# A macaron diffusion layer: side work of the first FFN handed out in small pieces, and the right-hand pools moved by 288 bytes

## The chip, the cores and the metric

One core of a Trainium2 chip runs the whole layer as one program. The metric is the device time of one execution in microseconds (us); three timed runs of the kernel before gave a median of 2588.1 us.

## What is computed

One layer works on 1024 latent tokens and 256 context tokens with 1024 features, all in float32: a half-step SwiGLU, then attention and a state-space branch (S5) side by side, then a second half-step SwiGLU for the latents, then a final norm. Each part is preceded by an RMS norm with a shift and a scale, and followed by a gate; the nine shift, scale and gate vectors come from a small product with the conditioning vector (adaLN).

```python
def swiglu(h, w_gu, w_down):
    gate, up = jnp.split(h @ w_gu, 2, axis=-1)
    return (jax.nn.silu(gate) * up) @ w_down
...
x = x + 0.5 * mx[2] * swiglu(modulate(x, g_ffn1[l], mx[0], mx[1]), w_gu1[l], w_down1[l])
ctx = ctx + 0.5 * mc[2] * swiglu(modulate(ctx, g_ffn1[l], mc[0], mc[1]), w_gu1[l], w_down1[l])
```

The S5 branch needs tables that depend on parameters alone (powers of the state matrix, input and output matrices). They can be made at any time before that branch.

## The kernel before

Every float32 product is made of three matmuls (mm3, L572): each operand is split into a high and a low part, and high x high, high x low and low x high are added in PSUM. ACT makes the high part, POOL the low part (split, L568).

**The first FFN** (ffn, L593) holds the transposed, normed tokens in three blocks: 512, 512 and 256 tokens (XB). Its hidden width of 2816 is walked in 22 slices f of 128. A slice does the gate product of all three blocks, then the up product of all three; a block of 512 is 24 matmuls of 512 columns, the third block 24 of 256. ACT takes the silu of a gate block out of PSUM (silu, L655), VectorE (DVE) multiplies the up block with it (act_of, L661), ACT and POOL split the result. The down products run at every second slice for two slices at once, between the gate and the up products: ten token tiles of 128, two halves each, six matmuls a half (120 in a phase), and DVE adds each half to the accumulator acc in SBUF (accum, L647). There are four PSUM banks with the tag gu and four with the tag dn. Slice 21 does the down products of slice 20 alone, three matmuls a half. The instructions of an engine run in program order.

**The side work.** A generator (gen in ffn1_mix_in, L820) makes, on DVE and POOL, the later adaLN vectors (adaln_rest, L178) and then the S5 tables (s5_pre, L246): small arithmetic first, then 16 cells (8 pairs of groups, 2 directions). A cell has six products on DVE (AB), six on POOL (M), a copy (rep), and the table T with 32 DVE operations. side (L581) advances the generator by one step, twice a slice: ahead of the gate products, and ahead of the up products. One step is four adaLN weight rows, or a whole cell. What needs PSUM and TensorE (PE) is put off with defer (L578): reduce and extract of adaLN, and finish of a cell (transposes s5p and products s5k on two dn banks, copies and some 17 DMA issues on ACT's queue); it runs at a later call of side.

**Scaling of the accumulator.** At slice 20, behind its down products, at (L829) multiplies all ten accumulator tiles by the gate (DVE), adds the input to five of them on POOL and, behind the up products, to the other five on DVE. From there on the down weights are multiplied by the gate when they are loaded (load, L599).

**Where the tiles lie.** Pools open from the left (upwards from address 0, where 1024 bytes are kept for DMA) or from the right (downwards). The allocator of the program of before gives these start addresses, in bytes of a partition: left, the weights of FFN 1 (78528, 82624, ...), the activations (53952, ...), FFN 2's first token block hH0, hL0 (45760, 62144) and its weights (87744, ...): all leave 192 when divided by 512. Right: big (147424), FFN 2's second token block hH1, hL1 (196576, 212960) and w_glu (133088): all leave 480. The tile big holds the tokens of FFN 1, later the keys and latents of attention, and both operands of the product with w_out (wo).

Of the kernel before, what the change touches and what calls it, by code (L numbers as in the profile page):

```python
# [41 lines left out]
XB = [(0, 4), (4, 4), (8, 2)]  # L42


class Kernel:
# [30 lines left out]
    def build(self):  # L76
        with self.tc.manual_schedule(), ExitStack() as st:
# [7 lines left out]
            sbig, srow, sattn = ExitStack(), ExitStack(), ExitStack()  # L85
            self.big = self.pool(sbig, "big", side="right").tile([128, 80 * 256], F32R, name="big")
# [91 lines left out]
    def adaln_rest(self, pool):  # L178
# [36 lines left out]
        def reduce(chunk, s, acc):  # L215
            p = [self.bank("dn", "adp") for _ in range(2)]
            for h in range(2):
                nc.tensor.matmul(p[h], lhsT=self.ones, rhs=acc[:, h * 512:(h + 1) * 512], start=True, stop=True)
            self.defer(0, lambda: extract(chunk, s, p))

        accs, grow = None, {}
        for i, (chunk, kt) in enumerate(jobs):
            sets = (0, 1) if chunk <= 4 else (0,)
            if i % 4 == 0:
                yield 5.0 * len(sets)
# [13 lines left out]
            if kt == KT - 1:  # L239
                for s in sets:  # L240
                    self.defer(0, lambda chunk=chunk, s=s, acc=accs[s]: reduce(chunk, s, acc))
        while self.late:
            yield 1.0


    def s5_pre(self, st):  # L246
# [14 lines left out]
        with ExitStack() as s0:  # L261
# [11 lines left out]
            def exp_parts(x, w, em=False):  # L273
# [5 lines left out]
                self.ts(q, r, 1.0 / 8, MUL, 1.0, ADD)  # L279
                for i in (7, 6, 5, 4, 3, 2):  # L280
                    self.tt(q, q, r, MUL)
                    self.ts(q, q, 1.0 / i, MUL, 1.0, ADD)
                self.tt(q, q, r, MUL)
# [10 lines left out]
            yield 6.0  # L294
            ld = sm("e4", 1)
            self.ts(ld[:, 0], par[:, 2, :], -87.0, ALU.max, 88.0, ALU.min)
            dt, _ = exp_parts(ld, 1)
# [10 lines left out]
            mg, em = exp_parts(x, 2, True)  # L308
            mag, em1 = mg[:, 0], em[:, 0]
            V.tensor_copy(self.r8, mg[:, 1])  # L310
            yield 6.0
# [11 lines left out]
            self.ts(v, t2, -1.0 / 132, MUL, 1.0, ADD)  # L323
            for ds, dv in ((72, 90), (42, 56), (20, 30), (6, 12)):
# [3 lines left out]
                self.ts(v, v, -1.0 / dv, MUL, 1.0, ADD)  # L328
            self.tt(s, s, th, MUL)
            self.tt(v, v, t2, MUL)  # L330
            self.ts(v, v, 0.5, MUL)
            for _ in range(2):
# [5 lines left out]
                self.ts(s, t, 2.0, MUL)  # L338
            cs = sm()
# [13 lines left out]
            V.reciprocal(out=den, in_=den)  # L353
            self.tt(fr, am1, lr, MUL)
# [7 lines left out]
            yield 6.0  # L362
# [7 lines left out]
            yield 6.0  # L370
# [8 lines left out]
            while m < NSEQ:  # L379
# [12 lines left out]
                m *= 2  # L392
            dv = lambda x: x.rearrange("p r t (c d g) -> p r t d c g", d=2, g=GC)
# [13 lines left out]

        for c in range(G // GC):
            mk = []
            for d in range(2):  # L410
                yield 6.4 if d else 7.8
                if d == 0:
# [7 lines left out]
                    tb = pool.tile([128, 2 * GC, CH], F32, tag="tb", name="tb")  # L420
                    self.ts(bW, bW, sgn, MUL)
# [3 lines left out]
                    self.tt(B2, bW, b8(fr), MUL)  # L425
                    self.tt(tb, bS, b8(fi), MUL)
                    self.tt(B2, B2, tb, SUB)
                    self.ts(C1, C1, sgn, MUL, -1.0, MUL)
                    self.ts(C2, C2, -1.0, MUL)
                gq = slice((c * 2 + d) * GC, (c * 2 + d + 1) * GC)  # L430
# [8 lines left out]
                def cross(nt, p, X, Y, first, second, tag, e):  # L439
                    ta = buf("ta" + tag, GC * 9 * CH, GC, nt, CH)  # L440
                    o1 = buf("o1" + tag, GC * 9 * CH, GC, nt, CH)
                    o2 = buf("o2" + tag, GC * 9 * CH, GC, nt, CH)
                    self.tt(o1, pv(p, 0, nt), bv(X, nt), MUL, e)
                    self.tt(ta, pv(p, 1, nt), bv(Y, nt), MUL, e)
                    self.tt(o1, o1, ta, ADD, e)
                    self.tt(o2, pv(p, first[0], nt), bv(first[1], nt), MUL, e)
                    self.tt(ta, pv(p, second[0], nt), bv(second[1], nt), MUL, e)
                    self.tt(o2, o2, ta, SUB, e)
                    return o1, o2
# [10 lines left out]
                for r in range(2):  # L460
                    V.tensor_copy(T[:, r, :, col(0, NB)], bsrc[:, r] if d == 0 else bsrc[:, r, :, ::-1])
                for l in range(5):
# [4 lines left out]
                             bb(lev[:, l, 0]), bb(lev[:, l, 1]), T[:, 0, :, col(m, m + ln)], T[:, 1, :, col(m, m + ln)])  # L467

# [35 lines left out]
                self.defer(0, finish)  # L504
# [10 lines left out]
            self.defer(2, fin2)  # L515
        while self.late:
            yield 1.0
# [60 lines left out]
    def defer(self, slots, fn):  # L578
        self.late.append([slots, fn])

    def side(self, budget):  # L581
        late, self.late = self.late, []
        for e in late:
            if e[0] <= 0:
                e[1]()
            else:
                self.late.append([e[0] - 1, e[1]])
        if self.gen is not None and self.cost <= budget:
            self.cost = next(self.gen, None)
            if self.cost is None:  # L590
                self.gen = None

    def ffn(self, blocks, hT, w_gu, w_dn, acc, P, hook=None, side=None, at=None, preload=None, keep=False, joint=False, start=None, pairs=0):  # L593
# [40 lines left out]
        def down(fs, tiles, post):  # L634
            for t in tiles:
                b = next(i for i, (t0, n) in enumerate(blocks) if t0 <= t < t0 + n)
                ts = slice((t - blocks[b][0]) * 128, (t - blocks[b][0] + 1) * 128)
                for half in range(2):
# [6 lines left out]
                    post(t, cs, p)  # L645

# [33 lines left out]
        for f in range(NF):  # L680
# [46 lines left out]
    def ffn1_mix_in(self, srow):  # L727
# [23 lines left out]
        with ExitStack() as sact:  # L751
            actp = self.pool(sact, "act")
            with ExitStack() as sw:
# [72 lines left out]
                self.gen, self.cost = gen(), 0.0  # L826
# [925 lines left out]
```

## Time and profile before

| | us |
|---|---|
| median of three runs | 2588.1 |
| lowest, highest | 2588.07, 2588.35 |
| the profiled execution's own time | 2585.26 |
| its span, first to last instruction | 2583.5 |

PE is busy for 2450.9 us of the span, DVE for 1580.0, POOL for 1091.8 and ACT for 810.9. The first FFN runs from about 62 to 1070 us of the span, the mixing part to 1830 (attention from about 1250), the second FFN to the end. In the profile a name before the arrow is the tile written, those behind it are the tiles read; L59 is the helper of all tensor_tensor operations, L574 to L576 are the three matmuls of mm3. The granted clock is given as a share of full speed.

### The profile page before, as it was taken

To read this page: it belongs to the slowest core of one execution; us is meant where nothing else is said; L and a number is where in the kernel's file an instruction comes from. 1 tells how busy PE (TensorE), PEld (TensorE's weight loads), DVE (VectorE), ACT (ScalarE), POOL (GpSimd) and SP (SyncE) were. 2 spreads that over 40 slices of the span, in tenths; PEclk is the share of its full clock that TensorE was granted. 3 is DMA by queue.
4 is the path that set the end of the run, shared out by engine and by line. 5 is a ranking of instruction groups with operands and counts; after the bars stand their busy time and mean duration, and the time that the engine had idled before them with its cause. 6 is when DMAs were issued, how large, how long until landed. Compare 5 with 4: busy or idle time off the path is not lost. (4 is left out here: it accounts for less than half of the span.)

```text
span 2583.5 us, 32552 instructions
## 1 busy us (share of the span) xinstructions
PE 2450.9 (95%) x12100; PEld 2004.9 (78%) x12100; DVE 1580.0 (61%) x2896; ACT 810.9 (31%) x1555; POOL 1091.8 (42%) x1010
## 2 busy tenths in 40 slices
PE   7999999999899898898899999989999999999998
PEld 3787888878777787697677778767788888888886
DVE  3567554597797768647788888872444444444443
ACT  4311111111121121533677777762411111111112
POOL 2432322254363355526566666665522233222222
PEclk9999999999999999999999999999999999999999
DMA  7233531122131232405100000014111111111111
GB/s 278 66 109 120 171 131 58 36 66 69 55 97 60 63 115 81 149 21 198 35 4 16 11 16 25 21 61 143 66 49 50 49 49 49 47 44 49 49 41 65
DMA packets 92894, 186.36 MB, mean 72 GB/s; under 512 B 23352, under 2 KB 53304, under 8 KB 91712
## 3 DMA queue, kind: packets, MB, share of 16 engines
q1 hardware_dynamic: 59984, 163.92, 18.9%
q10 hardware_dynamic: 32752, 20.36, 2.6%
q8 instruction: 95, 1.56, 0.2%
q14 instruction: 63, 0.52, 0.1%
HBM read 155.52 MB, written 27.54 MB: 71 GB/s over the span
## 5 line engine op out<-in xcount | busy, mean ns | idle before, releaser
L59 POOL TENSOR_TENSOR wL<-raw,wH 128x1024 fp32r<-128x1024 f32 x130 | 329.7, 2540 | 741.2 <-ACT wH L569 723.7
L59 DVE TENSOR_TENSOR acc<-dn,acc 128x512 f32<-128x512 f32 x556 | 377.5, 691 | 361.4 <-PE dn L576 361.1
L574 PE MATMUL gu<-big,wH 128*128 128x512 f32 (+1 forms) x1056 | 385.3, 365 | 9.1 <-DVE sg L59 6.5
L575 PE MATMUL gu<-big,wH 128*128 128x512 f32 (+1 forms) x1056 | 379.8, 360 | 1.2 <-POOL big L59 1.2
L576 PE MATMUL gu<-big,wL 128*128 128x512 f32 (+1 forms) x1056 | 379.6, 359 | 0.2 <-POOL wL L59 0.2
L574 PE MATMUL dn<-wH,aH 128*128 128x512 f32 x792 | 314.0, 396 | 29.4 <-DVE acc L59 28.3
L575 PE MATMUL dn<-wL,aH 128*128 128x512 f32 x792 | 311.6, 393 | 0.0
L576 PE MATMUL dn<-wH,aL 128*128 128x512 f32 x792 | 311.4, 393 | 0.1
L569 ACT ACTIVATE wH<-raw 128x1024 fp32r<-128x1024 f32 x130 | 136.3, 1054 | 490.9 <-DVE raw L59 227.6
L575 PE MATMUL gu<-hL,wH 128*128 128x512 f32 x704 | 276.5, 393 | 4.3 <-POOL hL L59 3.0
L574 PE MATMUL gu<-hH,wH 128*128 128x512 f32 x704 | 277.5, 394 | 0.0
L576 PE MATMUL gu<-hH,wL 128*128 128x512 f32 x704 | 276.3, 393 | 0.0
L59 POOL TENSOR_TENSOR aL<-sg,aH 128x512 fp32r<-128x512 f32 (+1 forms) x110 | 137.5, 1259 | 268.2 <-ACT aH L569 268.1
L59 DVE TENSOR_TENSOR sg<-gu,sg 128x512 f32<-128x512 f32 (+1 forms) x110 | 68.3, 635 | 292.3 <-PE gu L576 275.8
L574 PEld LDWEIGHTS gu<-big,wH 128*128 128x128 f32 x1056 | 200.5, 190 | 47.2 <-DVE sg L59 7.3
L575 PEld LDWEIGHTS gu<-big,wH 128*128 128x128 f32 x1056 | 200.4, 190 | 35.5 <-issue 1.7
L576 PEld LDWEIGHTS gu<-big,wL 128*128 128x128 f32 x1056 | 200.4, 190 | 33.4 <-POOL wL L59 0.6
L574 PEld LDWEIGHTS dn<-wH,aH 128*128 128x128 f32 x792 | 150.8, 190 | 63.8 <-DVE acc L59 31.4
L59 DVE TENSOR_TENSOR ptL<-pt,ptH 128x512 fp32r<-128x512 f32 x240 | 162.9, 686 | 52.7 <-ACT ptH L1344 52.2
L569 ACT ACTIVATE aH<-sg 128x512 fp32r<-128x512 f32 (+1 forms) x110 | 63.2, 588 | 405.8 <-DVE sg L59 399.7
L576 PEld LDWEIGHTS dn<-wH,aL 128*128 128x128 f32 x792 | 150.7, 190 | 33.1 <-POOL aL L59 0.5
L575 PEld LDWEIGHTS dn<-wL,aH 128*128 128x128 f32 x792 | 151.0, 191 | 31.2
(318 smaller groups left out, 4792.5 us busy)
## 6 DMA issues: line engine op xcount, KB each, us to landing
raw<-in_w_gu SPq DMA_DIRECT2D x86, 512.0 KB, 3.3
wmr<-in_w_mod SPq DMA_DIRECT2D x56, 512.0 KB, 4.3
raw<-in_w_down SPq DMA_DIRECT2D x44, 512.0 KB, 3.8
row<-d_s SPq DMA_DIRECT2D x16, 576.0 KB, 3.9
wm<-in_w_mod SPq DMA_DIRECT2D x8, 1024.0 KB, 7.9
d_s<-T ACTq DMA_DIRECT2D x32, 160.0 KB, 2.1
ck<-d_s SPq DMA_DIRECT2D x16, 320.0 KB, 3.7
acc<-in_x SPq DMA_DIRECT2D x8, 512.0 KB, 4.7
```

The source lines that it names most:

```text
L59: (eng or self.nc.vector).tensor_tensor(out=out, in0=a, in1=b, op=op)
L569: self.nc.scalar.activation(out=H, in_=raw, func=AF.Copy)
L574: mm(out, lhsT=AH, rhs=BH, start=start, stop=False)
L575: mm(out, lhsT=AH, rhs=BL, start=False, stop=False)
L576: mm(out, lhsT=AL, rhs=BH, start=False, stop=stop)
```

## The change

The generator now yields every few operations, each time with a cost. pump adds a credit and advances the generator until the credit is used up: 1.1 for each of a block's token tiles (4.4, 4.4, 2.2) behind every gate and up block, 1.0 behind every token tile of the down products. side only runs what was put off: behind gate blocks 0 and 1, ahead of the up products and behind each up block anything, elsewhere only what needs no new PSUM bank (extract). A generator that has named a put-off function as held is not advanced until that function has run. T of a cell comes ahead of M and AB. The scaling of the accumulator becomes such a generator from slice 20's up products to slice 21's gate products; what is left of it is drained ahead of slice 21's down products. A tile of 288 bytes is put at the right end, and the 1024 bytes at address 0 become 512: right pools lie 288 bytes lower, left pools 512.

```diff
@@ -40,6 +40,9 @@
+GURATE, DNRATE = 1.1, 1.0
+SCRATCH = 512
+PADR = 288
@@ -83,6 +86,7 @@ build
             sbig, srow, sattn = ExitStack(), ExitStack(), ExitStack()
+            self.pool(st, "padr", side="right").tile([128, PADR // 4], F32, name="padr")
             self.big = self.pool(sbig, "big", side="right").tile([128, 80 * 256], F32R, name="big")
@@ -216,13 +220,12 @@ adaln_rest
-            self.defer(0, lambda: extract(chunk, s, p))
+            self.defer(0, lambda: extract(chunk, s, p), False)
...
-            if i % 4 == 0:
-                yield 5.0 * len(sets)
+            yield 1.4 * len(sets)
...
             if kt == KT - 1:
                 for s in sets:
-                    self.defer(0, lambda chunk=chunk, s=s, acc=accs[s]: reduce(chunk, s, acc))
+                    fn = lambda chunk=chunk, s=s, acc=accs[s]: reduce(chunk, s, acc)
+                    self.defer(1, fn)
+                self.held = fn
+                yield 4.0
         while self.late:
-            yield 1.0
+            self.held = self.late[-1][1]
+            yield 0.0
@@ -277,9 +284,11 @@ s5_pre
...
+                yield 1.3
                 for i in (7, 6, 5, 4, 3, 2):
                     self.tt(q, q, r, MUL)
                     self.ts(q, q, 1.0 / i, MUL, 1.0, ADD)
+                    yield 0.5
...
+        last = None
         for c in range(G // GC):
             mk = []
             for d in range(2):
-                yield 6.4 if d else 7.8
...
+                    c = 0.7 if e is V else 0.0
                     self.tt(o1, pv(p, 0, nt), bv(X, nt), MUL, e)
+                    yield c
                     self.tt(ta, pv(p, 1, nt), bv(Y, nt), MUL, e)
+                    yield c
...
-                M1, M2 = cross(9, pwC, C1, C2, (0, C2), (1, C1), "m", Q)
-                AB, AB2 = cross(8, pwB, B1, B2, (1, B1), (0, B2), "a", V)
-                rep = buf("rep", GC * 128, GC, 8, CH)
-                V.tensor_copy(rep, bv(B1, 8))
                 T = pool.tile([128, 2, GC, NSEQ], F32, tag="T", name="T", bufs=2)
...
+                yield 0.6
                 for l in range(5):
...
+                    yield 1.4 + 0.01 * ln
+                if last:
+                    self.held = last if any(e[1] is last for e in self.late) else None
+                    yield 0.0
+                M1, M2 = yield from cross(9, pwC, C1, C2, (0, C2), (1, C1), "m", Q)
+                AB, AB2 = yield from cross(8, pwB, B1, B2, (1, B1), (0, B2), "a", V)
+                rep = buf("rep", GC * 128, GC, 8, CH)
+                V.tensor_copy(rep, bv(B1, 8))
+                yield 0.6
...
-                self.defer(0, finish)
+                self.defer(2, finish)
+                last = finish
...
-            self.defer(2, fin2)
+            self.defer(4, fin2)
@@ -575,20 +607,34 @@
-    def defer(self, slots, fn):
-        self.late.append([slots, fn])
-
-    def side(self, budget):
+    def defer(self, slots, fn, bank=True):
+        self.late.append([slots, fn, bank])
+
+    def side(self, banks=True):
         late, self.late = self.late, []
         for e in late:
-            if e[0] <= 0:
+            if not banks and e[2]:
+                self.late.append(e)
+            elif e[0] <= 0:
                 e[1]()
             else:
-                self.late.append([e[0] - 1, e[1]])
-        if self.gen is not None and self.cost <= budget:
-            self.cost = next(self.gen, None)
-            if self.cost is None:
+                self.late.append([e[0] - 1, e[1], e[2]])
+        self.held = self.held and any(e[1] is self.held for e in self.late) and self.held
+
+    def pump(self, credit):
+        self.credit = min(self.credit + credit, 4.0 + credit)
+        while self.gen is not None and self.credit > 0 and not self.held:
+            c = next(self.gen, None)
+            if c is None:
                 self.gen = None
+            else:
+                self.credit -= c
+
+    def drain(self):
+        while self.gen is not None or self.late:
+            self.side()
+            self.pump(1e9)
+        self.credit = 0.0
@@ -643,6 +689,8 @@ ffn, down (once a token tile)
                     post(t, cs, p)
+                self.pump(DNRATE)
+                self.side(False)
@@ -695,12 +743,15 @@ ffn, f > 0
-                if side:
-                    side(13.0)
                 sg = {}
                 for b in nblk:
                     sg[b] = silu(b, gu(f, 0, b))
+                    self.pump(blocks[b][1] * GURATE)
+                    if side:
+                        side(b < len(blocks) - 1)
                 load(f + 1, 0)
+                if at:
+                    at(f, -1)
...
                 if side and f < NF - 2:
-                    side(13.0)
+                    side()
                 for b in nblk:
                     act[b] = act_of(f, b, sg[b], gu(f, 1, b))
+                    self.pump(blocks[b][1] * GURATE)
+                    if side and f < NF - 2:
+                        side()
@@ -841,17 +894,23 @@ ffn1_mix_in, at(NF - 2, 0)
-                            while self.gen is not None or self.late:
-                                self.side(1e9)
+                            self.drain()
...
-                            self.xload = load
-                            for t in list(range(half, NT)) + list(range(half)):
-                                self.tt(acc[t], acc[t], g[int(t >= NX)], MUL)
-                                if t >= half:
-                                    self.tt(acc[t], acc[t], load(t), ADD, nc.gpsimd)
                             P["gates"] = [(g[0], actp), (g[1], self.fin)]
-                        else:
-                            for t in range(half):
-                                self.tt(acc[t], acc[t], self.xload(t), ADD)
-                            sxr.close()
-                            win(self.pool(swin, "winA", side="right"), 2)
+
+                            def prescale():
+                                yield 0.0
+                                for i in range(half):
+                                    for t in (half + i, i):
+                                        self.tt(acc[t], acc[t], g[int(t >= NX)], MUL)
+                                        yield 1.3
+                                    self.tt(acc[half + i], acc[half + i], load(half + i), ADD, nc.gpsimd)
+                                    self.tt(acc[i], acc[i], load(i), ADD)
+                                    yield 1.3
+
+                            self.gen = prescale()
+                    elif f == NF - 1 and phase == -1:
+                        self.drain()
+                        sxr.close()
+                        win(self.pool(swin, "winA", side="right"), 2)
@@ -1736,7 +1795,7 @@ kernel
-    nc = bacc.Bacc("TRN2", target_bir_lowering=False, num_devices=1, dynamic_dma_scratch_size=1024)
+    nc = bacc.Bacc("TRN2", target_bir_lowering=False, num_devices=1, dynamic_dma_scratch_size=SCRATCH)
```

## Rows read from the trace of the kernel before

**Rows 1.** The page: busy time, share of the span, instructions by engine.
```profile
PE 2450.9 (95%) x12100; PEld 2004.9 (78%) x12100; DVE 1580.0 (61%) x2896; ACT 810.9 (31%) x1555; POOL 1091.8 (42%) x1010
```
**Rows 2.** Windows by stage: PE, PEld, DVE, ACT, POOL busy (count), granted clock, DMA.
```profile
540.00:950.00 410.00, 379.26 (x1849) 316.09 (x1849) 344.59 (x809) 62.46 (x107) 189.23 (x197) 0.95 0.24 73
1250.00:1830.00 580.00, 546.94 (x2996) 442.70 (x2995) 434.42 (x694) 397.88 (x851) 374.00 (x441) 1.00 0.11 35
```
**Rows 3.** Waits of PE, 130 to 1200 us: total, times, longest, in us.
```profile
PE dn L574 <- DVE acc L59: 28.3, 8, 6.4
PE gu L574 <- DVE sg L59: 6.5, 1, 6.5
PE s5k L477 <- POOL o1m L59: 6.3, 3, 2.2
```
**Rows 4.** Timeline of PE, two down phases: start us, us of one, what.
```profile
484.70 0.39 PE L574 MATMUL dn<-wH,aH 128*128 128x512 f32 x1
...
511.92 0.40 PE L574 MATMUL gu<-big,wH 128*128 128x512 f32 x1
...
568.87 0.39 PE L574 MATMUL dn<-wH,aH 128*128 128x512 f32 x1
...
579.77 0.79 PE L574 MATMUL dn<-wH,aH 128*128 128x512 f32 x1 [5.28 <-DVE acc L59]
...
603.87 0.27 PE L473 MATMUL s5p<-ident,o1a 128*128 128x128 f32 x1
```
**Rows 5.** Windows behind two waits, columns as in rows 2.
```profile
580.00:584.00 4.00, 4.00 (x10) 3.13 (x11) 2.21 (x4) 0.00 (x0) 0.00 (x0) 0.50 0.00 0
652.00:656.00 4.00, 4.00 (x12) 3.14 (x12) 3.73 (x13) 0.00 (x0) 1.41 (x2) 0.60 0.08 17
```
**Rows 6.** Timeline of DVE and of POOL inside the waiting phase.
```profile
573.99 0.29 DVE L59 TENSOR_TENSOR TA<-T,lev 128x128 f32<-128x128 f32 x1
574.20 2.43 DVE L59 TENSOR_TENSOR TB<-T,lev 128x128 f32<-128x128 f32 x1
...
574.05 2.43 POOL L59 TENSOR_TENSOR wL<-raw,wH 128x1024 fp32r<-128x1024 f32 x1 [2.76 <-ACT wH L569]
```
**Rows 7.** Windows of tile acc, then of sg: PE, PEld, DVE busy, then DVE, ACT, POOL.
```profile
540.00:950.00 410.00, 0.00 (x0) 0.00 (x0) 54.18 (x80) 0.00 (x0) 0.00 (x0) 0.95 0.24 73
...
540.00:950.00 410.00, 14.70 (x27) 23.58 (x49) 28.94 (x24) 0.95 0.24 73
```
**Rows 8.** Timeline of PE, DVE and POOL in slices 20 and 21.
```profile
987.66 0.40 PE L574 MATMUL gu<-big,wH 128*128 128x512 f32 x1
...
1024.32 0.40 PE L574 MATMUL dn<-wH,aH 128*128 128x512 f32 x1
...
988.46 22.45 DVE L59 TENSOR_TENSOR acc<-acc,g 128x1024 f32<-128x1024 f32 x10
...
1026.13 12.82 DVE L59 TENSOR_TENSOR acc<-dn,acc 128x512 f32<-128x512 f32 x20
...
989.76 16.67 POOL L59 TENSOR_TENSOR acc<-acc,xr 128x1024 f32<-128x1024 f32 x5 [22.65 <-DVE acc L59]
```
**Rows 9.** Timeline of PE: first matmuls of successive blocks of 24; wo: the first and the 41st.
```profile
442.70 0.40 PE L574 MATMUL gu<-big,wH 128*128 128x512 f32 x1
...
448.30 0.40 PE L574 MATMUL gu<-big,wH 128*128 128x512 f32 x1
...
1955.32 0.39 PE L574 MATMUL gu<-hH,wH 128*128 128x512 f32 x1
...
1960.76 0.40 PE L574 MATMUL gu<-hH,wH 128*128 128x512 f32 x1
...
1966.37 0.40 PE L574 MATMUL gu<-hH,wH 128*128 128x512 f32 x1
...
1766.42 0.39 PE L574 MATMUL wo<-big 128*128 128x512 f32 x1
...
1775.49 0.39 PE L575 MATMUL wo<-big 128*128 128x512 f32 x1
```

More of the change, by code (lines that the diff above doesn't have):

```diff
@@ L292, in exp_parts @@
                 return s, e
-            yield 6.0
             ld = sm("e4", 1)
             self.ts(ld[:, 0], par[:, 2, :], -87.0, ALU.max, 88.0, ALU.min)
-            dt, _ = exp_parts(ld, 1)
+            dt, _ = yield from exp_parts(ld, 1)
             dt = dt[:, 0]
@@ L307, in s5_pre @@
             self.ts(x, x, -87.0, ALU.max)
-            mg, em = exp_parts(x, 2, True)
+            yield 1.8
+            mg, em = yield from exp_parts(x, 2, True)
             mag, em1 = mg[:, 0], em[:, 0]
             V.tensor_copy(self.r8, mg[:, 1])
-            yield 6.0
+            yield 1.8
             th, k = sm("e0"), sm("e1")
@@ L323, in s5_pre @@
             self.ts(v, t2, -1.0 / 132, MUL, 1.0, ADD)
+            yield 3.0
             for ds, dv in ((72, 90), (42, 56), (20, 30), (6, 12)):
@@ L328, in s5_pre @@
                 self.ts(v, v, -1.0 / dv, MUL, 1.0, ADD)
+                yield 1.0
             self.tt(s, s, th, MUL)
@@ L338, in s5_pre @@
                 self.ts(s, t, 2.0, MUL)
+                yield 1.2
             cs = sm()
@@ L353, in s5_pre @@
             V.reciprocal(out=den, in_=den)
+            yield 2.5
             self.tt(fr, am1, lr, MUL)
@@ L361, in s5_pre @@
             self.tt(fi, fi, den, MUL)
-            yield 6.0
+            yield 2.0
             for k in range(2, 9):
@@ L369, in s5_pre @@
                 self.tt(pw[:, 1, k, :], t, t1, ADD)
-            yield 6.0
+                yield 1.3
             wc, ws = sm(None, 1)[:, 0], sm(None, 1)[:, 0]
@@ L392, in s5_pre @@
                 m *= 2
+                yield 2.0
             dv = lambda x: x.rearrange("p r t (c d g) -> p r t d c g", d=2, g=GC)
@@ L420, in s5_pre @@
                     tb = pool.tile([128, 2 * GC, CH], F32, tag="tb", name="tb")
+                    yield 0.5
                     self.ts(bW, bW, sgn, MUL)
@@ L425, in s5_pre @@
                     self.tt(B2, bW, b8(fr), MUL)
+                    yield 1.5
                     self.tt(tb, bS, b8(fi), MUL)
@@ L429, in s5_pre @@
                     self.ts(C2, C2, -1.0, MUL)
+                    yield 1.5
                 gq = slice((c * 2 + d) * GC, (c * 2 + d + 1) * GC)
@@ L442, in cross @@
                     o2 = buf("o2" + tag, GC * 9 * CH, GC, nt, CH)
+                    c = 0.7 if e is V else 0.0
                     self.tt(o1, pv(p, 0, nt), bv(X, nt), MUL, e)
+                    yield c
                     self.tt(ta, pv(p, 1, nt), bv(Y, nt), MUL, e)
+                    yield c
                     self.tt(o1, o1, ta, ADD, e)
+                    yield c
                     self.tt(o2, pv(p, first[0], nt), bv(first[1], nt), MUL, e)
+                    yield c
                     self.tt(ta, pv(p, second[0], nt), bv(second[1], nt), MUL, e)
+                    yield c
                     self.tt(o2, o2, ta, SUB, e)
+                    yield c
                     return o1, o2
-                M1, M2 = cross(9, pwC, C1, C2, (0, C2), (1, C1), "m", Q)
-                AB, AB2 = cross(8, pwB, B1, B2, (1, B1), (0, B2), "a", V)
-                rep = buf("rep", GC * 128, GC, 8, CH)
-                V.tensor_copy(rep, bv(B1, 8))
                 T = pool.tile([128, 2, GC, NSEQ], F32, tag="T", name="T", bufs=2)
@@ L513, in fin2 @@
                     nc.scalar.dma_start(self.d_s5[q][:, O_K:O_K + 128], mk[0][:, g])
-            self.defer(2, fin2)
+            self.defer(4, fin2)
         while self.late:
-            yield 1.0
+            self.held = self.late[-1][1]
+            yield 0.0
     def rot(self, TA, TB, c, s, wc, ws, co, so):
@@ L824, in gen @@
                         yield from self.s5_pre(sg)
-                self.gen, self.cost = gen(), 0.0
+                self.gen, self.credit, self.held = gen(), 0.0, None
                 g = []
```

2 lines of the change are left out of this document (added).

## The prediction

> **What bounds the kernel now.** The page first: PE is busy 95% of the span [rows 1], so time goes away only where PE waits or where a matmul takes longer than it must. The windows by stage come next: the S5 part of the first FFN, 540 to 950 us, has the granted clock at 0.95 and PE busy 379 of 410 us, though DVE is busy 345 and POOL 189 [rows 2]: nobody is full, so work stands in the wrong order. The waits of PE name it: 28.3 us in down products waiting for DVE's acc, 6.5 us once in a gate/up block for sg, 6.3 us in three s5k products for POOL's o1m [rows 3].
>
> The timeline shows one such wait. A down phase of 120 matmuls takes 511.92 - 484.70 = 27.22 us; the one at 568.87 takes 35.00 [rows 4]. PE stands for 5.28 us, because acc comes behind a whole cell in DVE's order. And then it is slow: in 580 to 584 the clock is 0.50 [rows 5], the lower of its levels, 1.2 GHz, after PE had idled 5.3 us. So a wait costs more than the waits view says: here 7.8 us for 5.3. Four down phases are like this, of which one is shown; the other three take 35.53, 35.50 and 35.29 us between the same marks.
>
> **Part 1, the cells in pieces.** Removed: 35.00 + 35.53 + 35.50 + 35.29 - 4 x 27.22 = **32.4 us** of down phases [rows 4]. The s5k waits: finish now runs at the third call of side behind its cell, and POOL's six products of a cell lie at least two blocks back (8.4 us, a block of 24 being 5.60 us and the small one half [rows 9]); the 6.3 us go [rows 3], and with them the slow clock behind each of the three (0.60 in 652 to 656 [rows 5], so 0.8 x 4 / 2 = 1.6 us or a little more lost, taken as 1.8): **11.7 us**.
>
> Added: DVE instructions are the same ones, so the question is whether DVE keeps up. From 540 to 950 it has 344.6 us [rows 2], 54.2 of them acc and 14.7 sg [rows 7]; 275.7 are left for 16 cells, 17.2 each. By the yields a cell costs 13.9 credits, and a pair 3.5 more: 15.7 each, so a credit is 1.10 us of DVE, POOL's interference included (a DVE operation of 0.29 us takes 2.43 when POOL's weight split begins first [rows 6]). The up products of a slice hand out 11 credits, 12.1 us; with 1.7 us of sg that is 13.8 of PE's 14.0. Gate products: 12.1 of 14.0. A token tile of a down phase: 1.1 plus two acc of 0.68 (54.18 / 80 [rows 7]) is 2.46 of 2.72. DVE is close to full but never over, and lag is covered: a gate/up PSUM bank is needed again four blocks later, a dn bank after four halves of 1.36 us, 5.4 us. Following the credits through the code, cells run from slice 8 to 18, the generator ends in slice 19, so the drain of slice 20 has nothing to do; adaLN's last reduce falls into slice 6; held keeps the down phases of slices 10, 14 and 16 free of cell work. SP's queue: the weight rows and bc are issued piece by piece instead of four at once, with the same tiles to wait for. ACT's 17 DMA issues of a finish move only from one block end to another. I charge **5 us** for late pieces (ends: 0, and 20, which is two and a half phases like that of rows 4; nearer the low end, because three of those same phases have DVE idle half the time).
>
> **Part 2, scaling the accumulator.** From 987.66 to 1024.32 the up and gate products of slices 20 and 21 take 36.66 us [rows 8] for four times 5.60 plus halves, 28.0: 8.6 us lost. DVE's ten multiplications take 22.45 us while POOL adds five tiles in 16.67, and DVE is at work from 988.46 to 1026.13 without a pause [rows 8]. The change moves this work between the blocks but must end it ahead of slice 21's down products, and DVE then has nothing to do while it waits for the first up block. 37.7 us of DVE still stand against 28 of PE plus four banks of 0.68. The wait goes, and what is late next is slice 21's first down product, by 37.7 - 28.0 - 2.7 = 7 us, plus 1 to 2 of slow clock: the same 8.6. I take **0**; ends: 8.6 won if spreading ends the interference, 6 lost if DVE idles for the first block.
>
> **Part 3, the pools.** A block of 24 gate matmuls takes 5.60 us in FFN 1 (442.70 to 448.30), but 5.44 us in FFN 2 for the first token block and 5.61 for the second [rows 9], with the same weights, count and clock, over and over. The first block's operands lie at addresses that leave 192 over 512, moving and stationary alike; the second block and all of FFN 1 have the moving operand at 480 and the stationary one at 192. It is not the right side as such: wo has both operands in big, both at 480, and takes 9.07 us for 40, 0.227 each [rows 9]; the down products of FFN 1 (both at 192) have 27.22 / 120 = 0.227 [rows 4]. So matmuls go at 0.227 us where the operands agree and at 0.2335 where they differ by 288, and the change makes 480 - 288 = 192 everywhere (512 on the left changes nothing). FFN 1 has 22 x 2 x 2 = 88 blocks of 512: 88 x 0.16 = 14.1, less 0.6 for the four blocks ahead of the wait of part 2, which DVE sets: **13.5 us**. FFN 2 has 44 on the right: 44 x 0.15 (the next pair of blocks gives 5.47 and 5.60) = **6.6 us**. Third blocks of 256 columns: 0 (ends 0 and 3, half the gain of each of 1056). Attention: 3 x 192 score products of 512 columns (two for each of 96 units of a head and 128 queries) times 0.0065 is 3.7 at most, and some 180 projections 1.2; PE waits for others there in 33 of 580 us [rows 2], so **2** (ends 0 and 5). The sum is 22.1.
>
> The Trainium skill (TensorE: Matmul & The Clock Gate, the section "Wait — 56ns, not 53.3ns?") knows start-to-start of warm back-to-back matmuls as columns over 2.4 GHz plus a fixed 2.5 ns, 215.7 ns for 512 columns, with no term for where an operand lies. By that rule the pools are worth nothing and the sum is 22.1 us less; the rows show both paces above its figure, and two of them.
>
> **Sum.** 32.4 + 11.7 - 5 + 0 + 22.1 = 61.2 us. The profiled execution, 2585.3 us (span 2583.5), becomes 2524.1. The median of the runs, 2588.1, is 2.8 above it: **2527 us**.
>
> **Rivals.** (a) *The pools do nothing*: the two paces come from something else that differs between the two token blocks. Against it: wo, which is fast with both operands where the slow ones have one [rows 9]. For it: no trace here has moved a tile. 2527 + 22 = 2549 us. Chance 0.15. (b) *DVE falls behind in every slice*, slower than before: the up products leave it 0.2 us of 14.0, and if pieces cost 1.3 us a credit instead of 1.10 (POOL's split meeting every piece as in [rows 6]), up and gate products of a slice together lag by 2.3 us more than they catch up. Past 5.4 us, four dn banks, which three slices are enough for, each of nine down phases waits as the four do now, 8.1 us with the clock: 73 us, against 44.1 + 22.1 won: 2588 + 7 = 2595. For it: up products at 98% load. Against it: the same work fits into nine slices now with 66 us of DVE idle [rows 2]. Chance 0.06. (c) *The generator isn't done by slice 20* (held costs it more turns than I count) and the drain sets the rest down in a lump: each cell left over is 17.2 us of DVE ahead of an up block, 9 us of PE; two cells, 2545. Chance 0.07. The forecast itself: 0.72, with a range of its own from 2510 (no late pieces, part 2 won, attention 5) to 2541 (late pieces 15, part 2 4 lost).
>
> Range: down to 2510, and up to 2554 to take in (a) and (c). A measurement of this kernel tells 0.2%, 5 us, from no change. Faster 0.91, within 0.03, slower 0.06.
>
> **What would show it.** In the trace after: no wait of PE for acc in slices 8 to 18 and a granted clock of 1.00 there; down phases of 27.2 us; s5k without a wait; a wait of some 7 us at the start of slice 21's down products instead of in slice 20; 24 gate matmuls in 5.44 us in both FFNs. Wrong would be: gate blocks still at 5.60 (a); DVE without idle time and waits in every down phase (b); a lump of cell work behind slice 20's down products (c).

## The result, and the profile after

The kernel is slower: 2617.8 us (2614.8 to 2625.6, four runs) against 2588.1, a ratio of 1.0121 [1.0097, 1.0145]. The forecast was 2527, so 91 us are to be found. The profiled execution took 2620.3 us (span 2618.5). The page's first line of the kernel after, and the windows of two stages (columns as in [rows 2]):

```profile
PE 2443.3 (93%) x12100; PEld 2015.4 (77%) x12100; DVE 1545.1 (59%) x2896; ACT 811.8 (31%) x1555; POOL 1072.8 (41%) x1010
...
130.00:440.00 310.00, 293.50 (x1383) 239.48 (x1382) 221.43 (x401) 43.83 (x62) 77.27 (x38) 0.99 0.36 116
540.00:950.00 410.00, 362.01 (x1769) 304.63 (x1768) 265.66 (x673) 60.67 (x101) 168.51 (x183) 0.94 0.22 69
```

PE's busy time was to grow in the second stage; it fell from 379 us to 362 [rows 2]. DVE isn't the reason, for it works less there than before, 266 us for 345. And PE now idles 16 us from 130 to 440, where before it was busy for all 310. The waits of PE, 130 to 1200 us (answering to [rows 3]), and one row of the waits of DVE, 98 to 1100:

```profile
PE dn L606 <- DVE acc L62: 52.6, 12, 19.7
PE s5k L507 <- POOL o1m L62: 17.4, 2, 8.7
PE adp L222 <- DVE ad L69: 5.3, 5, 2.3
PE gu L608 <- POOL wL L62: 3.9, 3, 1.7
...
PE gu L606 <- ACT wH L601: 2.8, 2, 1.4
```
```profile
DVE bc L66 <- DMA bc<-in_s5bc: 77.7, 6, 16.7
```

Waits for acc and o1m did not go: they are 1.9 and 2.8 times what they were. Waits for ad, wL and wH are new. Behind the longest stands the row of DVE, which the waits of DVE before don't have at all: DVE waits 77.7 us for bc, six times. The timeline follows one such wait back (ACT, POOL, SP, DVE, PE; a q behind an engine marks a DMA that it issues, a bracket gives the engine's idle time just before and what ended it, and line numbers shift a little from kernel to kernel):

```profile
794.53 5.10 ACTq L529 DMA_DIRECT2D K<-R  x8
799.68 1.06 ACT L601 ACTIVATE wH<-raw 128x1024 fp32r<-128x1024 f32 x1 [6.08 <-DMA K<-R]
...
800.81 2.34 POOL L62 TENSOR_TENSOR wL<-raw,wH 128x1024 fp32r<-128x1024 f32 x1 [9.54 <-ACT wH L601]
803.11 0.70 POOL L62 TENSOR_TENSOR o1m<-pwC,bc 128x288 f32<-128x288 f32 x1
...
805.95 0.70 POOL L62 TENSOR_TENSOR tam<-pwC,bc 128x288 f32<-128x288 f32 x1
...
806.68 0.55 SPq L428 DMA_DIRECT2D bc<-in_s5bc  x1
...
809.30 0.26 DVE L66 TENSOR_SCALAR bc<-bc,sgn 128x64 f32<-128x64 f32 x1 [16.66 <-DMA bc<-in_s5bc]
...
817.19 0.79 PE L606 MATMUL dn<-wH,aH 128*128 128x512 f32 x1 [19.67 <-DVE acc L62]
```

Read it from the top. ACT issues the eight copies of a finish and only then splits the next weights. POOL's half of that split waits 9.5 us, and POOL's six products M of the cell stand behind it. The last of them that reads bc (its C half) ends at 806.65, and bc has one buffer, so SP issues the next pair's bc at 806.68. DVE has waited 16.7 us by then, with the adds of the down phase queued behind the cell: PE stands for 19.7. Five in-order queues pass one delay on. Before, M stood at the head of its cell and the next bc half a slice later, and DVE's waits have no bc. That the new order is what took the slack is read from the code and this row; no run put M alone back ahead of T.

Slices 20 and 21, answering to [rows 8] (timeline of PE):

```profile
1025.65 0.39 PE L606 MATMUL gu<-big,wH 128*128 128x512 f32 x1
...
1053.18 0.40 PE L606 MATMUL dn<-wH,aH 128*128 128x512 f32 x1
...
1068.23 0.79 PE L606 MATMUL dn<-wH,aH 128*128 128x512 f32 x1 [12.14 <-DVE acc L62]
...
1081.32 0.39 PE L606 MATMUL gu<-big,wH 128*128 128x512 f32 x1
```

The two sets take 27.53 us instead of 36.66, without a wait; the down products behind them 28.14 instead of 13.74, since PE stands 12.1 us at their fifth half, when the four dn banks are used up. Nothing fell into slice 20's drain.

### The profile page after: what moved, and what is told of

The parts are those of the page before. It is cut to its first block, busy times and chain, and to the rows that moved or that the text cites. A ratio compares the mean times of both kernels' runs of the same rounds, so it can differ in the third digit from the quotient of the medians.

```text
span 2618.5 us, 32564 instructions
## 1 busy us (share of the span) xinstructions
PE 2443.3 (93%) x12100; PEld 2015.4 (77%) x12100; DVE 1545.1 (59%) x2896; ACT 811.8 (31%) x1555; POOL 1072.8 (41%) x1010
## 5 line engine op out<-in xcount | busy, mean ns | idle before, releaser
L62 POOL TENSOR_TENSOR wL<-raw,wH 128x1024 fp32r<-128x1024 f32 x130 | 315.4, 2430 | 763.8 <-ACT wH L601 745.5
```

The costliest lines, as they stand in the source:

```text
L62: (eng or self.nc.vector).tensor_tensor(out=out, in0=a, in1=b, op=op)
```

## The experiments

The kernel before ran beside every set of experiments (medians 2585.0 to 2587.5); kernels of different sets are compared by their ratios to it, times 2588. The changed kernel and the first four runs are compared by their medians, since the kernel before agreed to 0.6 us there (2588.1 and 2587.5). An interval reaches 2 to 4 us to either side, so smaller differences say little.

**The pools alone.** `pads_only` is the kernel before with

```diff
+            self.pool(st, "padr", side="right").tile([128, 288 // 4], F32, name="padr")
-... dynamic_dma_scratch_size=1024)
+... dynamic_dma_scratch_size=512)
```

> The kernel before with the two pool moves alone (288 bytes on the right, 512 instead of 1024 at address 0); the side work as before. Theory (paces follow the operands' addresses): blocks of 24 gate matmuls take 5.45 us in both FFNs and the time is 2588 - 22 = 2566 us, 2560 to 2570. Rival (the two paces came from something else): 2588 us, blocks still at 5.60 us. Third: nearly all of the pace is won but DVE's lump waits grow with it, 2570 to 2580.

Measured: 2573.5, ratio 0.9945 [0.993, 0.9959]: 14 us faster. A gate set (first matmuls of its first 512-column block, of its 256-column block, and of what follows; PE's timeline), in pads_only and then, from the same set's 256-column block on, in the kernel before, where it begins at 442.70 [rows 9]:

```profile
439.72 0.40 PE L575 MATMUL gu<-big,wH 128*128 128x512 f32 x1
...
450.63 0.28 PE L575 MATMUL gu<-big,wH 128*128 128x256 f32 x1
...
453.50 0.40 PE L575 MATMUL gu<-big,wH 128*128 128x512 f32 x1
```
```profile
453.90 0.28 PE L574 MATMUL gu<-big,wH 128*128 128x256 f32 x1
...
456.70 0.40 PE L574 MATMUL gu<-big,wH 128*128 128x512 f32 x1
```

48 wide matmuls take 10.91 us; before, 11.20. Over all of FFN 1 their mean distance falls from 0.2333 to 0.2274, in FFN 2 from 0.2304 to 0.2267. But 24 narrow ones take 2.87 instead of 2.80 (0.1196 for 0.1169). By 1049.37, where FFN 1's last down phase begins (1053.28 before), only 3.9 us are won: the waits of [rows 3] are all still there (27.8, 7.7 and 7.1 us), and a PE that comes to them sooner waits longer. From slice 2's down phase to slice 12's PE gains 4.2 us (430.5 for 434.6); from there to slice 18's, the stage of the four long waits, it loses 1.4 (299.0 for 297.6).

**bc in two halves.** `bc_split` is the changed kernel with

```diff
-bc = pool.tile([128, 4, 2 * GC, CH], F32, tag="bc", name="bc")
-nc.sync.dma_start(bc, a["s5bc"][:, :, ...])
+bc = pool.tile([128, 2, 2 * GC, CH], F32, tag="bc", name="bc")
+nc.sync.dma_start(bc, a["s5bc"][:, 0:2, ...])
+cc = pool.tile([128, 2, 2 * GC, CH], F32, tag="cc", name="cc", bufs=2)
+nc.sync.dma_start(cc, a["s5bc"][:, 2:4, ...])
```

so that the half that DVE reads no longer waits for POOL, and the half that POOL reads has two buffers.

> The changed kernel with the tile bc cut in two: the B half as before, the C half (read last by POOL's M products) in two buffers, so that its load need not wait for POOL's M of the cell before. Theory A (DVE waits for bc, bc's load for POOL's M, M behind a weight split that waits for ACT, ACT behind the DMA issues of finish): DVE's 77.7 us of waiting for bc fall below 10, PE's 17.4 us for o1m and 52.6 us for acc in slices 8 to 18 lose most, some 14 us at slice 21 stay; time 2575 us, between 2560 and 2590. Theory B (DVE is simply too full when work comes in pieces): at most 10 us better than 2618, the waits of PE for acc stay.

Measured: 2585.3, ratio 0.999 [0.9981, 1.0]. DVE's waits for bc are gone. The waits of PE, 130 to 1200:

```profile
PE dn L609 <- DVE acc L62: 23.0, 8, 12.1
PE s5k L510 <- POOL o1m L62: 16.8, 2, 8.4
PE adp L222 <- DVE ad L69: 6.8, 5, 2.2
```

The chain through bc cost 32.6 us, all of the loss and a little more. The s5k waits don't depend on it.

**The scaling as before.** `old_scaling` is the changed kernel, and `bc_split_old_scaling` is bc_split, with the lump in slice 20 put back:

```diff
-                            def prescale():
...
-                            self.gen = prescale()
-                    elif f == NF - 1 and phase == -1:
...
+                            for t in list(range(half, NT)) + list(range(half)):
+                                self.tt(acc[t], acc[t], g[int(t >= NX)], MUL)
+                                if t >= half:
+                                    self.tt(acc[t], acc[t], load(t), ADD, nc.gpsimd)
...
+                        elif phase == 1:
+                            for t in range(half):
+                                self.tt(acc[t], acc[t], self.xload(t), ADD)
```

> The changed kernel with the scaling of the accumulator in two lumps as before (slice 20). Forecast's part 2 (the wait only moves): PE's 12.1 us at slice 21's first down product go and some 7 us for sg in slice 20 come back; time 2618 less 0 to 6. Rival (pieces help there): 2618 plus 5 to 9.

> Both edits: theory A and a wait that only moves give bc_split less 0 to 6 us, about 2571. If B holds, 2610.

Measured: 2611.4 (1.0092 [1.0075, 1.0109]) and 2579.3 (0.9969 [0.9956, 0.9982]). Handing out the scaling costs 6.4 and 6.0 us; it adds to the bc chain and doesn't meet it. The fine cells as such now do what they were to do: the down phases of slices 12 to 18 take 28.4, 28.1, 29.6 and 28.5 us. Yet pads_only, without any pieces, is faster by 6.

**adaLN in lumps again.** `ada_lumps` is bc_split_old_scaling with four jobs at each of the two old places and the reduction at the next (the calls at these places are not shown):

```diff
-            yield 1.4 * len(sets)
+            if i % 4 == 0:
+                yield 5.0 * len(sets)
...
-                    self.defer(1, fn)
-                self.held = fn
-                yield 4.0
+                    self.defer(0, fn)
```

> On top of bc_split_old_scaling, adaLN alone goes back to lumps: four jobs at each of the two old places of a slice, the reduction at the next place; the S5 pieces stay. Theory A: the fine adaLN pieces are what lets PE idle for 16.4 us from 130 to 440 (reductions waiting for DVE's ad, late weight splits, and the slow clock behind each), so the down phase of slice 8 begins near 397 as in pads_only instead of 414.66, and the time is 2579.3 - 17.7 = 2561.6 (2557 to 2567). Rival B: the lateness only moves: adaLN ends a slice and a half later, the cells run into the drain of slice 20, and the time stays at 2575 or more. PE's waits for ad: 0 to 1 us by A.

Measured: 0.9936 [0.9922, 0.9951], 8.5 us faster. Both happened. Slice 8's down phase begins at 397.01 instead of 414.66 (PE's timeline of ada_lumps, then of bc_split_old_scaling), and PE is busy 309.5 of 310 us from 130 to 440:

```profile
397.01 0.40 PE L608 MATMUL dn<-wH,aH 128*128 128x512 f32 x1
```
```profile
414.66 0.40 PE L609 MATMUL dn<-wH,aH 128*128 128x512 f32 x1
```

So by then the fine adaLN pieces have cost 17.7 us. The lumps have the last four of adaLN's 40 matmuls still ahead of them there (slice 8's down phase takes 28.5 us with them, for 27.2), which leaves 16. But the cells end later, too (a row of PE's waits and one of DVE's timeline):

```profile
PE gu L608 <- DVE sg L62: 21.6, 1, 21.6
...
980.09 12.69 DVE L62 TENSOR_TENSOR acc<-acc,g 128x1024 f32<-128x1024 f32 x10 [15.67 <-DMA g<-d_gate]
```

The finishes of two cells fell into slice 20's drain, and the gate that the scaling needs was loaded behind them. From slice 20's down phase to slice 21's it takes 90.8 us, in bc_split_old_scaling 63.5: 27 us are lost there, 14.7 of them in the longer wait for sg (21.6 for 6.9), the rest mostly in slice 20's own down phase (38.7 for 27.2).

**The finish's DMAs on SP's queue.** In `finish_sp` (on bc_split_old_scaling) and `ada_lumps_finish_sp` (on ada_lumps) the issues of finish read

```diff
-                        nc.scalar.dma_start(...)
+                        nc.sync.dma_start(...)
```

> On top of bc_split_old_scaling, the 17 DMA issues of each finish go to SP's queue instead of ACT's. Theory A: POOL's M stands behind a weight split that waits for ACT's half of it, and ACT's half stands behind the finish's issues (10 us of ACT's queue); without them the two s5k waits of 8.4 us shrink to under 2 each, and with the slow clock behind them 15 to 20 us go: 2562 (2558 to 2566). Rival B: M is late because it is issued behind T, whatever ACT does: the s5k waits stay and the time is 2579 (2576 to 2582). Rival C: SP, in order, now holds the weight loads behind K<-R and o2m, and PE waits for weights: 2585 or more, new waits of ACT for raw.

> Both of the edits. If they don't meet each other, the gains add: 2561.6 - 17 = 2544 (2538 to 2552), below pads_only's 2573.5 and so the fastest so far. If the cells run into slice 20's drain, or SP's queue holds the weights, it is above the better of the two alone.

Measured: 1.0032 [1.002, 1.0043] and 1.0042 [1.0025, 1.0059], 16 and 27 us slower than without. Theory A fell, rival C held. The timeline (SP, ACT, POOL, PE):

```profile
561.45 5.06 SPq L532 DMA_DIRECT2D K<-R  x8
566.55 0.58 SPq L652 DMA_DIRECT2D raw<-in_w_gu  x1
...
570.19 1.06 ACT L604 ACTIVATE wH<-raw 128x1024 fp32r<-128x1024 f32 x1 [9.66 <-DMA raw<-in_w_gu]
...
571.33 2.38 POOL L62 TENSOR_TENSOR wL<-raw,wH 128x1024 fp32r<-128x1024 f32 x1 [10.48 <-ACT wH L604]
...
575.95 0.58 PE L510 MATMUL s5k<-o1m,rep 128*128 128x128 f32 x1 [9.85 <-POOL o1m L62]
```

ACT is free, but now the weight itself is loaded behind the same eight copies. The delay is in their place ahead of the weights, not in the engine that issues them.

**The pad at another distance.** `pads_160` is pads_only with 160 bytes instead of 288.

> pads_only with a right pad of 160 bytes instead of 288: the right pools then lie at 320 over 512, the left ones at 192, so moving and stationary operands of FFN 1's gate and up products differ by 128 instead of 0. Theory A (the pace follows from whether the two residues agree): 512-column gate matmuls stay at 0.233 us, 256-column ones at 0.117, and the time is that of the kernel before, 2588 (2584 to 2591). Rival B (288 is bad in itself, any other distance is good, or the move as such helps): 0.2274 and 2573 (2571 to 2577).

Measured: 0.9993 [0.9984, 1.0002], no change. The same gate set as above:

```profile
442.65 0.40 PE L575 MATMUL gu<-big,wH 128*128 128x512 f32 x1
...
453.82 0.28 PE L575 MATMUL gu<-big,wH 128*128 128x256 f32 x1
```

Its 48 wide matmuls take 11.17 us; over all of FFN 1 they stay at 0.2326 (FFN 2: 0.2300). Theory A stands for them; the narrow ones went to 0.1192 all the same.

**The cells a slice earlier, and without the pad.** `ada_lumps_fast` gives adaLN's chunks 5 and 6 eight jobs a lump; `ada_lumps_fast_nopads` is that without padr.

```diff
-            if i % 4 == 0:
+            if kt == 0 or kt == 4 and chunk not in (5, 6):
```

> ada_lumps with adaLN's chunks 5 and 6 (one set each) handed out in lumps of eight jobs instead of four, so that the cells begin one slice sooner. Theory: what ada_lumps lost is the last cells running into slice 20, where the gate's load stood behind them in SP's queue and PE waited 21.6 us for sg instead of 6.9; with the cells done ahead of it, 14.7 us go: 2568.6 - 14.7 = 2554 (2546 to 2558), ratio to before near 0.988. Rival: eight jobs at once are 10 us of DVE ahead of silu and their rows come at 2.5 us each, so PE waits for sg or acc near 330 to 400: 2562 or more.

> The same without the 288 bytes on the right (the left stays where it was, the residues are 480 and 192 again). By the paces counted over whole phases (gate and up: 0.2333 to 0.2274 for 512 columns, but 0.1169 to 0.1197 for 256; FFN 2: 0.2304 to 0.2267) the pools are worth 44 x (48 x 0.0059 - 24 x 0.0028) = 9.5 and 2112 x 0.0037 = 7.8, in all 17 us where DVE isn't the bound: 17 us (14 to 20) above ada_lumps_fast. By the forecast's 22: 22. If what pads_only showed is all there is: 14 or less.

Measured: 0.994 [0.9925, 0.9955] and 0.9993 [0.9984, 1.0002]. The first was a miss: slice 20's wait is 6.9 us again, but eight jobs at once hold up a reduction for 4.5 us (slice 6's down phase begins at 321.51, with ada_lumps at 311.19), and two down phases wait 4 us each for acc. The second is 14.2 us slower: the pools are worth 14 us in pieces as in lumps, not 17 and not 22. Of these, 5.0 lie ahead of FFN 1's last down phase (1044.04 against 1049.04).

**The finish a block later.** `finish_late`, on bc_split_old_scaling:

```diff
-                self.defer(2, finish)
+                self.defer(3, finish)
...
-            self.defer(4, fin2)
+            self.defer(5, fin2)
```

> bc_split_old_scaling with each finish one call of side later (a block, 5.45 us). Theory: the two s5k waits of 8.4 us are a matter of where a finish falls against POOL's weight split, which stands ahead of M and waits for the finish before it; M comes at the same time as before, so the waits shrink by a block each, to about 3, and with the slow clock behind them the time is 2579.3 - 13 = 2566 (2562 to 2570). Rival: the chain moves along, since the weight split waits for the finish before, which is a block later too: waits still 8, cells end later, 2579 or more.

Measured: 0.9927 [0.991, 0.9944], 10.9 us faster. PE's waits, 130 to 1200:

```profile
PE dn L609 <- DVE acc L62: 12.2, 8, 5.5
...
PE s5k L510 <- POOL o1m L62: 1.0, 1, 1.0
```

The two waits of 8.4 us were a matter of where a finish falls against POOL's weight split. 5.1 us of new waits of down products for ACT's copy of s5k took some of it back.

**The reductions later, with higher rates.** `late_reduce`, on finish_late:

```diff
-GURATE, DNRATE = 1.1, 1.0
+GURATE, DNRATE = 1.2, 1.1
...
-                    self.defer(1, fn)
+                    self.defer(2, fn)
...
-                yield 1.3
+                yield 2.0
...
-                yield 2.0
+                yield 2.6
```

> finish_late with adaLN's reductions one call later (the pieces stay fine), the prices of two kinds of S5 preparation nearer to their time on DVE (1.3 to 2.0 and 2.0 to 2.6), and the rates 1.2 and 1.1 so that the cells still end ahead of slice 20. What is open is which of two things the fine adaLN pieces cost most by. Theory A: by the reductions, which stand on PE and wait for DVE's ad (6.4 us and the slow clock behind each): they go, slice 8's wait of 5.5 for acc shrinks too, the down phase of slice 6 begins near 318 instead of 330.74, and the time is 2565.4 - 18 = 2547 (2542 to 2553). Theory B: by the weight loads, which stand in SP's queue behind five to seven row loads that wait for DVE: the waits for ACT's wH and POOL's wL near 290 stay, the down phase of slice 6 begins at 325 or later, and the time is 2555 to 2563. Rival C: at the rate of 1.2 DVE falls behind in the cells and PE waits for acc in most down phases: 2570 or more.

Measured: 0.9989 [0.998, 0.9999], 16 us slower than finish_late. The waits for ad grew to 8.4 us, and the down phases of slices 10 to 18 wait 2.0, 6.1, 1.9, 6.1 and 2.0 us for acc: at these rates DVE falls behind, adaLN included. With three things changed at once it could not say what adaLN costs by; the next two change one thing each, and the third has both.

**adaLN's two costs apart.** `reduce_late` is finish_late with `self.defer(2, fn)` alone. `raw_ahead` is finish_late with the load of each raw weight tile issued one load ahead, and `raw_ahead_reduce_late` has both:

```diff
-            r = P["raw"].tile([128, 1024], F32, tag="raw", name="raw")
-            nc.sync.dma_start(r, ...)
+            r = raws.pop((f, which), None) or fetch(f, which)
...
             wt[f, which] = out
+            nxt = {0: (f - 1, 2), 1: (f + 1, 0), 2: (f + 1, 1)}[which]
+            if side and "gates" not in P and nxt not in wt and 1 <= nxt[0] < NF:
+                raws[nxt] = fetch(*nxt)
```

What it moves, in bc_split_old_scaling (SP, ACT, PE): a weight stands behind seven rows of adaLN that each wait for a buffer of DVE's, and its split comes late.

```profile
273.02 12.34 SPq L191 DMA_DIRECT2D wmr<-in_w_mod  x7
285.41 0.42 SPq L652 DMA_DIRECT2D raw<-in_w_gu  x1
...
292.19 1.06 ACT L604 ACTIVATE wH<-raw 128x1024 fp32r<-128x1024 f32 x1 [9.61 <-DMA raw<-in_w_gu]
...
293.30 0.58 PE L609 MATMUL gu<-big,wH 128*128 128x512 f32 x1 [1.76 <-ACT wH L604]
```

> finish_late with adaLN's reductions one call of side later, and nothing else (rates as there). Theory A (the reductions waiting for ad are the cost of the fine pieces): the waits for ad fall from 6.4 to under 2 and slice 6's down phase begins near 320 instead of 330.74 (311.2 in lumps). Theory B (the weight loads behind the rows): it begins at 327 or later, with the waits for wH and wL near 290 as they were. The whole time isn't the test here, since the cells end up to a slice later and may run into slice 20: 2556 to 2585.

> finish_late with each raw weight tile's load issued one load earlier (behind the load before it, half a slice ahead), so that it no longer stands in SP's queue behind the row loads and bc; the splits stay where they are. Theory B: the waits for wH and wL (3.3 and 1.6) go, with the slow clock behind them 6 to 10 us; slice 6's down phase begins near 323, and the time is 2565.4 - 8 = 2557 (2552 to 2561). Theory A: the splits were never the cost; the start stays at 329 or later and the time at 2562 to 2568. Rival C: the early load needs its buffer sooner, and SP now holds rows and bc behind a load that waits for POOL's wL: 2570 or more, waits for ad grow.

> Both of the edits. If the two make up the cost of the fine pieces, slice 6's down phase begins by 316, near the 311.2 of the lumps; if the rows themselves come too late for DVE (it stood 9.7 us for them), it stays above 322. The whole time: 2545 to 2560 if the cells end ahead of slice 20, up to 2580 if not.

Measured: 0.9988 [0.9979, 0.9997], 0.9871 [0.9855, 0.9888] and 0.9916 [0.9901, 0.9931]. The first down products of slices 6 and 8 in finish_late, in reduce_late and in raw_ahead:

```profile
330.74 0.40 PE L609 MATMUL dn<-wH,aH 128*128 128x512 f32 x1
...
414.82 0.40 PE L609 MATMUL dn<-wH,aH 128*128 128x512 f32 x1
```
```profile
325.64 0.40 PE L609 MATMUL dn<-wH,aH 128*128 128x512 f32 x1
...
418.36 0.40 PE L609 MATMUL dn<-wH,aH 128*128 128x512 f32 x1
```
```profile
325.49 0.40 PE L609 MATMUL dn<-wH,aH 128*128 128x512 f32 x1
...
409.57 0.40 PE L609 MATMUL dn<-wH,aH 128*128 128x512 f32 x1
```

With both edits they come at 320.36 and 412.85, in lumps at 311.19 and 397.01. At slice 6 each edit seems worth 5 us and the two to add. But with the reductions later, 28 of adaLN's 40 matmuls lie ahead of that mark and not 36, and eight of them take 3.0 us of PE (slice 4's down phase in lumps, 30.3 for 27.2). At slice 8 all 40 are done in these four kernels: the weights ahead are worth 5 us there, and with the reductions later the mark comes 3.5 and 3.3 us later. (By slice 10's, reduce_late is 5 us ahead of finish_late, 500.68 for 505.77: slice 8's phase takes 27.2 us there and not 35.0, but its first cell ends 33 us later.) So theory B holds for 5 us, theory A isn't borne out, and some 11 us of the pieces are neither. In raw_ahead PE still waits 7.6 us from 130 to 410 for ad, for acc and for another tile of DVE's (grow); that these waits and the slow clock behind them are the rest is not shown. Later reductions also push the cells into slice 20 (sg: 17.1 us in reduce_late), and in the whole time reduce_late is 16 us slower than finish_late. With the weights ahead the same split comes at 283.85 instead of 292.19, and the windows of raw_ahead show what the change was to bring:

```profile
540.00:950.00 410.00, 403.50 (x2045) 342.67 (x2044) 261.35 (x685) 69.95 (x116) 184.54 (x191) 1.00 0.25 76
```

raw_ahead takes 2554.2 us (2549.9 to 2556.6), 1.3% less than the kernel before, and is the fastest here. What its early weight loads would give the kernel before, with its lumps, was not run.

## Why the prediction was wrong

**The step that failed** is a sentence of Part 1: on SP's queue "the weight rows and bc are issued piece by piece", "with the same tiles to wait for". The tiles are the same, but not what stands ahead of them. For bc the tile is freed by POOL's M, which had moved from the head of the cell to behind T: 32.6 us (bc_split). For the weights, the rows of adaLN stand between them one by one: 5 us there, 8 by FFN 1's last down phase (1039.06 in finish_late, 1030.82 in raw_ahead), and 14.5 in the whole time by the ratios; their medians differ by 11, their profiled executions by 7. I charged 5 us for all late pieces. That M's new place is what made bc late is argued from the order; that bc was late, and what it cost, is shown.

**adaLN** has no term in the sum at all; I only asked when its last reduction falls. Its pieces cost some 16 us, in a stretch (130 to 440) where PE had no waits before.

**The s5k waits** (11.7 us to be won) stayed, 6.3 us before and 17.4 after. I put POOL's products two blocks back by the order of issue; POOL comes to them behind a weight split that waits for the finish before. finish_late won 10.9.

**The down phases** (32.4 us to be won): right, once bc is out of the way. The four take 114.6 us in bc_split_old_scaling, against 4 x 27.22 = 108.9; 5.7 over, where 5 were charged. The price of a credit, 1.10 us, and "close to full but never over" fit: at the rates of the change DVE keeps up, in late_reduce, at 1.2 and 1.1, no longer, as rival (b) has it. Rival (b)'s 2595 came near in size, but not by its mechanism: DVE was idle. Rival (c) didn't occur in the change; ada_lumps shows its price, 27 us for the finishes of two cells, where I had 18 for two cells.

**Part 2**: the wait came where it was put, in slice 21's down products behind their four banks, but at 12.1 us instead of 7. DVE starts the scaling only behind the first up block, at 1031.97, 6.3 us after the up products begin (0.8 us before, [rows 8]): that is the end of "6 lost". It also waits three times for xr, 4.7 us together, which I hadn't looked at: ten tiles go through three buffers. The part costs 6 instead of 0.

**Part 3**: mechanism right, size off. Where operands agree the pace is 0.2274; at a distance of 128 (pads_160) it stays at 0.2326, so rival (a) is out. The Trainium skill's rule (TensorE: Matmul & The Clock Gate, "Wait — 56ns, not 53.3ns?"), by which the pools were worth nothing, gives 215.7 ns for 512 columns wherever the operands lie; it does not hold here, where the traces show 227.4 and 233.3 ns. The term of 22.1 us measured 14. FFN 2, from its first gate product to its last down phase, gave 8.6 us, for 6.6 (714.5 to 705.9 from the kernel before to pads_only, the same in the ada_lumps_fast pair). The part between, with attention, gave nothing of its 2: it takes 2.5 and 0.3 us more (782.4 to 784.9, 782.3 to 782.6). FFN 1 gave 4 to 5, for 13.5. There, by the means, the two wide blocks of a set gain 0.28 us and not 0.32, the narrow block, put at 0, loses 0.07, and so 44 sets give about 9; the rest goes into the waits of slices 12 to 20, which a faster PE meets sooner.

The ledger of the 91 us, an estimate in which each item comes from one pair of kernels: bc 32.6, adaLN 16, s5k 10.9, pools 8, scaling 6, and slice 8's wait for acc behind S5's preparation 7.8 (35.0 for 27.2 in bc_split_old_scaling, where DVE works without a pause on S5's preparation until acc at 425.07; it is 27.9 in late_reduce, with dearer yields, but also 27.2 in reduce_late with the old ones, so the price isn't shown to be the reason). That is 82; some 9 us of short waits, with the slow clock behind them, stay unassigned, and of adaLN's 16 the cause of some 11 stays open.

## What to carry to other kernels

When work is cut into pieces and reordered, the time of its instructions can be the smaller part, as here. Write down, for each in-order queue, what now stands ahead of what, and for each single-buffered tile who frees it and what that engine has queued before; a chain of five queues turned a gain into a loss here. Issue loads of what PE needs ahead of loads that must wait for a buffer. And a faster matmul is worth its full sum only in the stretches that PE itself sets.

## What the runs showed of the hardware

The pace of a 512-column matmul depended on where its operands lie, at a granted clock of 1.00: 0.2274 us where stationary and moving operand leave the same remainder over 512, 0.2326 at a distance of 128, 0.2333 at 288. Other distances were not run. I had not expected that 256-column ones go the other way: 0.1169 at 288, 0.1192 at 128, 0.1196 where they agree. No run here explains either.
